# One-core hybrid decoder block: small weights side by side, score, split and evacuation steps reordered, and some of the last stage's stores and loads put on GpSimd's queue

## The chip, the cores and the metric

The kernel runs on one core of a Trainium2 chip. A core has TensorE (PE, matrix products; PEld is its weight load), VectorE (DVE), ScalarE (ACT), GpSimd (POOL) and SyncE (SP, which here only issues transfers). Each runs its own instructions in order and waits for the others by semaphores. Transfers issued from the queues of SP, ACT and POOL run on the same 16 DMA engines. The metric is the time of one execution in microseconds (us). Shapes below are partitions x elements.

## The reference

1040 tokens (16 meta tokens and 1024 of x) of width 1024 go through one layer, in float32:

```
h = h + mixer_block(rms_norm(h, norm_mix), ...)
h = h + conv_ffn(rms_norm(h, norm_ffn), w_up, conv_w, conv_b, w_down)
return rms_norm(h, norm_final)[16:]
```

mixer_block projects h with w_in into queries, keys and values of four GLA heads and four mLSTM heads, 24 small columns (g_lr, 16 wide, from which the GLA decay is made; m_i and m_f, 4 each), output gates and branch gates. A GLA head is gated linear attention, `scores[t,s] = sum_k q[t,k] k[s,k] exp(b[t,k] - b[s,k])` for s <= t, with b the running sum of the log decay, in chunks; an mLSTM head is a matrix memory with its own gates. The heads' outputs are normed, gated, multiplied with a branch weight each, merged and multiplied with w_out. conv_ffn is a gated MLP of width 2816 with a causal convolution of width 3 over tokens.

## The kernel before

Every float32 operand of a large product is split into a high part (a copy of ACT into float32r, H) and a low part (a subtraction of DVE or POOL, L); a product is three matmuls, HH, HL and LH, added up in PSUM. A scheduler places each engine's instructions by priorities (`hp`, and the order in which the code issues them); `tc.issue_after(x)` puts an instruction behind x.

**Projections and heads.** `key_query_proj(s)` and `value_proj(s)` give head s's matmuls (tiles pj and pv) in steps, and after each step `advance` lets the heads' own work (`gla`, `post`, ...) take a step. The 24 small columns come first: w_lr holds their weights, high and low apart, each padded to 128 columns; TensorE multiplies them in three thirds of the tokens by `proj_cm` (L160), three matmuls for each of 8 k, and ACT puts each third into raw_s with a bias. `pre` (L630) multiplies raw_s for the decay; DVE makes the running sums b (tile bc).

**Scores.** In `gla` the off-diagonal scores of a head are made in levels of block size b = 1, 2, ..., 64. `level(b)` builds a tile pk (differences on DVE, L742 and L743; Exp on ACT, L744; products on POOL and DVE, L746 and L747). `scores_small(pk, b)` multiplies it on TensorE (sc, L696), and DVE copies the result under a mask into A (L713). The list `made` keeps levels that were built and not yet multiplied: a level is multiplied when two newer ones are built. `diagonal` gives kq (L661), whose product with ones (L667) are the scores inside small blocks; sct (L686) turns A.

**Post.** `post(s, ...)` scales the head's output o, transposes it on TensorE (ot, L604), has ACT evacuate it to `of` (L606), and stores it. Head 0's post runs while head 1's levels are built.

**FFN up.** The up product goes over pairs q of 128 gate and 128 up columns and two pieces p of the tokens, in a Strassen-like scheme with 7 products on 2 x 2 blocks; `piece` (L1035 by way of `product`) adds them up in the banks V, X, Y and Z; u2raw (L1064) is the evacuation of X's sum on ACT. `prep_pair` splits the weights (A, L1451 and L1452, is one of its blocks). `combos(i)` builds the token blocks from hT: Br holds plain blocks, Bt the sums T; both are split (BH1r, BL1r, BH1t, BL1t: L1432 on ACT, L1433 on DVE; the 1 is the piece p = i // 2). `gate_pair(q)` convolves, gates and stores the result (rows adr, in sums for the down product), on SP's queue, for the last pair on ACT's.

**FFN down.** 44 steps i: round r (half of the tokens), phase ph (0: four products, 1: three), and row pair m. `fill(i)` loads a raw weight block (rd), its sums tdn, prepared earlier by POOL, and adr, and splits each into places do, dy, db, dw; `ahead` keeps four steps loaded ahead. All these loads go through `transfer`, which keeps them in order on SP's queue:

```
def transfer(dst, s):
    with tc.issue_after(queued[0].ins) if queued else nullcontext():
        queued[:] = [nc.sync.dma_start(dst, s)]
```

The four rows accs (4 x 128 x 1024) hold h (stored before as hsc) and take the sums from PSUM (DVE, L1780), half in `middle` behind phase 0, half in `finish` behind phase 1. `scaled` norms them: squares on ACT (sqj, L1796), the inverse root on POOL (fr, L1803), the product with gfin on DVE (L1808), the scaling on ACT (L1809), the store to out (L1811). Round 0's rows are scaled early in round 1 (`later`), before `load_acc(1)` loads the rows of round 1 into the same accs.

Of the kernel before, what the change touches and what calls it, by code (L numbers as in the profile page):

```python
# [45 lines left out]
def hybrid_kernel(ctx, tc, x, meta, norm_mix, w_in, b_in, gla_w_gate, gla_b_gate, gla_norm,  # L46
# [40 lines left out]

    rooted = []

# [24 lines left out]

    lr2 = hd.tile([P, 2, NK, P], F32R, name="w_lr", tag="v", bufs=2)
    nc.vector.memset(lr2.bitcast(F32), 0.0)
    lrHL = [lr2[:, i] for i in range(2)]
    SMALL = ((0, O_LR, 16), (32, O_MI, 4), (64, O_MF, 4))

    def prep_small():  # L120

        raw = wp.tile([P, T], F32, name="wr_lr", tag="gst", bufs=1)[:, :NK * 24].rearrange("p (k n) -> p k n", k=NK)
        wH, wL = lrHL
        at = 0
        for p0, off, n in SMALL:
            nc.sync.dma_start(raw[:, :, at:at + n], w_in[:, off:off + n].rearrange("(k p) n -> p k n", p=P))
            h = wH[:, :, p0:p0 + n]
            nc.scalar.activation(h, raw[:, :, at:at + n], AF.Copy)
            nc.vector.tensor_tensor(wL[:, :, p0:p0 + n], raw[:, :, at:at + n], h.bitcast(F32), OP.subtract)
            at += n  # L130
        return wH, wL

# [453 lines left out]
    def post(s, o, om, sc, ncols):  # L586
# [12 lines left out]
        for j in range(2):  # L599
            of = hd.tile([P, T], F32, name=f"of{s}_{j}", tag="r", bufs=2)  # L600
            for gi in range(2):
# [3 lines left out]
                a, b = 2 + 512 * gi, 2 + 512 * (gi + 1)  # L605
                nc.scalar.activation(of[:, a:b], tp.rearrange("p n w -> p (n w)"), AF.Copy, scale=ncols[j])  # L606
                if gi == 0:
# [35 lines left out]
    def gla(s):  # L643
# [74 lines left out]
        def level(b):  # L718
# [24 lines left out]
            nc.vector.tensor_tensor(pl, b4[:, :, 1, :], ref, OP.subtract)  # L743
            nc.scalar.activation(pk[:, :SEQ], pk[:, :SEQ], AF.Exp, scale=1.0 / 16)  # L744
            for eng, (e, k, _) in zip((nc.gpsimd, nc.vector), early):
# [670 lines left out]
    def combos(i):  # L1416

        p, c0 = i // 2, 128 * (i % 2) + (2 if i == 1 else 0)
        o, w = (0, 130) if i == 0 else (2, 128)
        A, B = hT[1 + i][:, :, o:130], hT[5 + i][:, :, o:130]  # L1420
        t12, t34 = (rb.tile([P, 8, 130], F32, name=f"T{g}_{i}", tag=f"T{g}")[:, :, :w] for g in (12, 34))
        nc.vector.tensor_tensor(t12[:, 0:4], B[:, 0:4], A[:, 0:4], OP.subtract)
        nc.vector.tensor_tensor(t12[:, 4:8], B[:, 4:8], t12[:, 0:4], OP.subtract)
        nc.vector.tensor_tensor(t34[:, 0:4], B[:, 4:8], B[:, 0:4], OP.subtract)
        nc.vector.tensor_tensor(t34[:, 4:8], A[:, 4:8], t12[:, 4:8], OP.subtract)
        jobs = ((Br, 0, 8, A), (Br, 8, 4, B[:, 4:8]), (Bt, 0, 8, t12), (Bt, 8, 8, t34))
        if i == 3:
            jobs = ((Br, 0, 8, A), (Bt, 0, 4, t12[:, 0:4]), (Bt, 8, 4, t34[:, 0:4]), (Bt, 4, 4, t12[:, 4:8]),
                    (Br, 8, 4, B[:, 4:8]), (Bt, 12, 4, t34[:, 4:8]))
        for dst, r0, n, src in jobs:  # L1430
            h = dst["H", p][:, r0:r0 + n, c0:c0 + w]
            nc.scalar.activation(h, src, AF.Copy)  # L1432
            x = nc.vector.tensor_tensor(dst["L", p][:, r0:r0 + n, c0:c0 + w], src, h.bitcast(F32), OP.subtract)  # L1433
            parts.append(x)

# [62 lines left out]
    def gate_pair(q):  # L1498
# [12 lines left out]
        m = q // 2  # L1511
        eng = nc.sync if q < NJ - 1 else nc.scalar

# [157 lines left out]

    def fill(i, pl, weights=True):

# [12 lines left out]
        jobs.append((pl.aH, pl.aL, pl.aL.bitcast(F32), (1024, 768)[ph], adr[ph][m][r].rearrange("p j c -> p (j c)")))  # L1686
        for h, l, raw, n, s in jobs:
            h, l, raw = h[:, :n], l[:, :n], raw[:, :n]
            if s is not None:
                transfer(raw, s)  # L1690
            nc.scalar.activation(h, raw, AF.Copy)
            nc.vector.tensor_tensor(l, raw, h.bitcast(F32), OP.subtract)
# [95 lines left out]
    def finish(r, j):  # L1788
# [17 lines left out]
        def scaled(i):  # L1806
# [3 lines left out]
            t = 4 * i + 2 * r + j  # L1810
            nc.sync.dma_start(out[P * t:P * (t + 1), :], acc[i])  # L1811

# [35 lines left out]

    AHEAD, PRI_F = 4, 100
    fetched = FIRST  # L1850
    kept = {}

    def ahead(i):
        nonlocal fetched
        while fetched < min(i + 1 + AHEAD, len(seq)):
            r, ph, m = seq[fetched]
            with hp(PRI_F):
                pl = ring[0](fetched)
                again = (r, ph) == (1, 0) and m in KEPT
                if again:  # L1860
                    pl.wH, pl.wL = kept[m]
                fill(fetched, pl, not again)
                used[fetched] = pl
# [12 lines left out]
    while i < len(seq):  # L1876
# [7 lines left out]
        if later and k == 2:  # L1884
# [51 lines left out]
```

## Time and profile before

| | |
|---|---|
| median of 3 runs | 1888.07 us (1885.97 to 1889.87) |
| profiled execution | 1888.81 us, its span 1887.1 us |
| busy | PE 1857.6 us, DVE 1217.3, ACT 869.0, POOL 403.5 |
| DMA | 270.02 MB in the span, mean 143 GB/s |

The profile's page has the busy time of each engine and its costliest groups; the list of waits says for which engine and line another one waited; windows give each engine's busy time, the granted clock of TensorE, the share of the DMA engines and GB/s in a stretch; timelines give start, duration, engine, line, operation, out<-in, and in brackets the idle time before and its releaser.

### The profile page before, as it was taken

To read this page: it belongs to the slowest core of one execution; us is meant where nothing else is said; L and a number is where in the kernel's file an instruction comes from. 1 tells how busy PE (TensorE), PEld (TensorE's weight loads), DVE (VectorE), ACT (ScalarE), POOL (GpSimd) and SP (SyncE) were. 2 spreads that over 40 slices of the span, in tenths; PEclk is the share of its full clock that TensorE was granted. 3 is DMA by queue.
4 is the path that set the end of the run, shared out by engine and by line. 5 is a ranking of instruction groups with operands and counts; after the bars stand their busy time and mean duration, and the time that the engine had idled before them with its cause. 6 is when DMAs were issued, how large, how long until landed. Compare 5 with 4: busy or idle time off the path is not lost.

```text
span 1887.1 us, 32610 instructions
## 1 busy us (share of the span) xinstructions
PE 1857.6 (98%) x13305; PEld 1775.2 (94%) x13305; DVE 1217.3 (65%) x1806; ACT 869.0 (46%) x1389; POOL 403.5 (21%) x447
## 2 busy tenths in 40 slices
PE   8999999999999999999999999999999999999998
PEld 8989999999999999999999999999999999987876
DVE  7666658454552465665442547688787887887767
ACT  5454555545553433432422335543443443455665
POOL 5401101205320001133281600012322222100100
PEclk9999999999999999999999999999999999999999
DMA  5211021143332856565983743324333334298794
GB/s 176 73 37 56 16 71 48 35 127 98 97 100 79 213 121 160 149 185 156 325 247 108 232 141 129 118 85 129 117 102 112 109 107 130 76 324 328 258 376 173
DMA packets 223361, 270.02 MB, mean 143 GB/s; under 512 B 13742, under 2 KB 179136, under 8 KB 223211
## 3 DMA queue, kind: packets, MB, share of 16 engines
q1 hardware_dynamic: 202907, 202.03, 34.8%
q0 software_dynamic: 16160, 55.65, 9.1%
q10 hardware_dynamic: 4144, 10.26, 1.6%
q8 instruction: 104, 1.70, 0.4%
q14 instruction: 46, 0.38, 0.1%
HBM read 198.33 MB, written 69.57 MB: 142 GB/s over the span
## 4 chain that ended last, share of the span: by engine, by line
PE 82%; DVE 7%; DMA 6%; ACT 2%; issue 2%; POOL 0%; SPq 0%; POOLq 0%; DVEq 0%; ACTq 0%
PE pj L163 11%; PE pv L206 7%; PE Xu L1035 6%; PE Yu L1035 6%; PE Zu L1035 6%; PE bg L1270 5%; PE bm L1270 5%; PE Xg L1035 4%; PE Yg L1035 4%; PE po L1557 4%; PE Zg L1035 4%; PE Vu L1035 3%; PE Vg L1035 2%; PE pdX L1712 1%; PE pdY L1712 1%
## 5 line engine op out<-in xcount | busy, mean ns | idle before, releaser
L513 POOL TENSOR_TENSOR ts<-ts 128x256 f32<-128x256 f32 x88 | 78.2, 894 | 49.4 <-DMA ts<-in_ffn_w_down_dram 47.0
L1470 POOL TENSOR_TENSOR SB<-SA,rg 128x512 f32<-128x512 f32 x20 | 31.8, 1588 | 238.0 <-issue 123.7
L206 PE MATMUL pv<-wH_mv,xH 128*128 128x256 f32 x256 | 74.8, 292 | 0.1
L206 PE MATMUL pv<-wH_gv,xH 128*128 128x256 f32 x256 | 74.4, 291 | 0.0
L746 POOL TENSOR_TENSOR pk<-pk,kT 128x256 f32<-128x256 f32 (+1 forms) x24 | 31.0, 1293 | 196.6 <-ACT pk L744 145.7
L1557 PE MATMUL po<-wH_wo,yH 128*128 128x256 f32 x256 | 72.7, 284 | 0.1
L206 PE MATMUL pv<-wL_gv,xH 128*128 128x256 f32 x256 | 72.1, 281 | 0.0
L206 PE MATMUL pv<-wL_mv,xH 128*128 128x256 f32 x256 | 72.0, 281 | 0.0
L206 PE MATMUL pv<-wH_mv,xL 128*128 128x256 f32 x256 | 72.0, 281 | 0.0
L1557 PE MATMUL po<-wL_wo,yH 128*128 128x256 f32 x256 | 71.7, 281 | 0.3 <-DVE wL_wo L112 0.3
L206 PE MATMUL pv<-wH_gv,xL 128*128 128x256 f32 x256 | 72.0, 281 | 0.0
L1557 PE MATMUL po<-wH_wo,yL 128*128 128x256 f32 x256 | 72.0, 282 | 0.0
L1505 DVE SCALAR_TENSOR_TENSOR cv<-u,fc,cv 128x1024 f32<-128x1024 f32 x44 | 65.2, 1485 | 0.4
L1452 POOL TENSOR_TENSOR A<-u2raw,A 128x512 fp32r<-128x512 f32 x20 | 43.8, 2192 | 90.4 <-ACT A L1451 90.4
L1270 PE MATMUL bg<-ogL,wH_bg 128*128 128x342 f32 x192 | 61.5, 320 | 0.0
L1270 PE MATMUL bm<-omH,wH_bm 128*128 128x342 f32 x192 | 61.4, 320 | 0.0
L1270 PE MATMUL bg<-ogH,wL_bg 128*128 128x342 f32 x192 | 61.4, 320 | 0.0
L1270 PE MATMUL bg<-ogH,wH_bg 128*128 128x342 f32 x192 | 61.4, 320 | 0.0
L1270 PE MATMUL bm<-omH,wL_bm 128*128 128x342 f32 x192 | 61.3, 319 | 0.0
L1270 PE MATMUL bm<-omL,wH_bm 128*128 128x342 f32 x192 | 61.2, 319 | 0.0
L1803 POOL TENSOR_TENSOR fr<-fv,mhalf 128x1 f32<-128x1 f32 x8 | 8.6, 1072 | 226.3 <-DVE fv L1800 137.4
L210 DVE TENSOR_TENSOR v<-pv,bB 128x256 f32<-128x256 f32 x64 | 26.7, 419 | 45.5 <-PE pv L206 45.1
(767 smaller groups left out, 7516.5 us busy)
## 6 DMA issues: line engine op xcount, KB each, us to landing
gw<-in_w_in_dram SPq DMA_DIRECT2D x26, 512.0 KB
ts<-in_ffn_w_down_dram POOLq DMA_DIRECT2D x44, 256.0 KB, 4.0
tdn<-ts POOLq DMA_DIRECT2D x44, 256.0 KB, 3.1
rg<-in_ffn_w_up_dram SPq DMA_DIRECT2D x22, 512.0 KB
ru<-in_ffn_w_up_dram SPq DMA_DIRECT2D x22, 512.0 KB
adr<-s SPq DMA_DIRECT2D x40, 256.0 KB
rd<-in_ffn_w_down_dram SPq DMA_DIRECT2D x20, 512.0 KB
do<-tdn SPq DMA_DIRECT2D x18, 512.0 KB
```

Of the source, the lines that this page charges most:

```text
L163: nc.tensor.matmul(pt[:, :n], a[:, k, :], b[:, k, base + t0:base + t0 + n], start=(i == 0), stop=(i == 3 * NK - 1))
L206: nc.tensor.matmul(pt[:, :DV], a[:, k, t0:t0 + P], b[:, k % 4, :], start=(i == 0), stop=(i == 3 * NK - 1))
L210: nc.vector.tensor_tensor(vt[:n, c, :DV], pt[:n, :DV], bB[:n, :], OP.add)
L513: nc.gpsimd.tensor_tensor(t[:, o], t[:, a], t[:, b], OP.subtract)
L746: eng.tensor_tensor(e, e, k, OP.mult)
L1035: nc.tensor.matmul(out[:, :n], x[:, k, :], y[:, k, :], start=start and k == 0 and j == 0, stop=stop and k == 3 and j == 2, skip_group_chec ...
L1270: nc.tensor.matmul(pt[:, i, :n], a[:, k, :], b[k][:, base + t0:base + t0 + n], start=(k == 0 and j == 0), stop=(k == NK - 1 and j == 2))
L1452: eng.tensor_tensor(l, src, h.bitcast(F32), OP.subtract)
L1470: late.tensor_tensor(sb[:, 0:4], sa[:, 0:4], rg[:, 0:4], OP.subtract)
L1505: nc.vector.scalar_tensor_tensor(y, u[:, j:SEQ + j], fc[:, j, jj:jj + 1], y, OP.mult, OP.add)
L1557: nc.tensor.matmul(pt[:, :DV], a, b[:, k % 4, :], start=(k == 0 and i == 0), stop=(k == NK - 1 and i == len(terms) - 1))
L1712: nc.tensor.matmul(banks[r, j, b], p, q, start=first and k == 0, stop=last and k == 2, skip_group_check=True)
```

## The change

- **Small weights**: w_lr is one tile with the high parts in columns 0 to 63 and the low parts in 64 to 127 (`small_proj`). For each k one matmul of all 128 columns with xH gives both products, one of the first 64 with xL the third. ACT copies the lower half of PSUM to raw_s, DVE adds the upper half and the bias. m_f's four rows move from 64 to 36, and a transfer on POOL's queue copies them to 64.
- **Scores**: for s = 0 a level is multiplied when three newer ones are built.
- **Exponentials**: for head 1 the Exp of the levels stands behind head 0's evacuation `of`.
- **Combos**: for piece 1 the plain block A is split before the sums T are built.
- **Queues**: the last pair's stores go to POOL's queue instead of ACT's; gfin is loaded after the second kept step of round 1 instead of in round 0; in round 0 accs is loaded one row per fill (steps 7 to 10); in round 1 accs is loaded on POOL's queue, and round 0's rows are stored to out there.

```
-    lr2 = hd.tile([P, 2, NK, P], F32R, name="w_lr", tag="v", bufs=2)
+    lr2 = hd.tile([P, NK, P], F32R, name="w_lr", tag="v", bufs=2)
...
-    SMALL = ((0, O_LR, 16), (32, O_MI, 4), (64, O_MF, 4))
+    SMALL = ((0, O_LR, 16), (32, O_MI, 4), (36, O_MF, 4))
...
+    def small_proj():
+
+        U.get(uk["lr"])
+        for t0, n in TH_ALL:
+            pt = ps.tile([P, 512], F32, name=f"plr{t0}", tag="pj", bufs=3)
+            for k in range(NK):
+                first, both = (xL, 64), (xH, P)
+                for j, (x, m) in enumerate((both, first) if k < NK - 1 else (first, both)):
+                    nc.tensor.matmul(pt[:m, :n], lr2[:, k, :m], x[:, k, t0:t0 + n],
+                                     start=(k == 0 and j == 0), stop=(k == NK - 1 and j == 1), skip_group_check=True)
+            with hp(PRI_E):
+                r = raw_s[0:64, t0:t0 + n]
+                nc.scalar.activation(r, pt[64:128, :n], AF.Copy)
+                nc.vector.scalar_tensor_tensor(r, pt[0:64, :n], bsm[0:64], r, OP.add, OP.add)
+            yield
+        nc.gpsimd.dma_start(raw_s[64:68, :], raw_s[36:40, :])
...
-                yield from proj_cm(uk["lr"], TH_ALL, 0, lambda p, t0, n: nc.scalar.activation(
-                    raw_s[0:96, t0:t0 + n], p[0:96, :], AF.Identity, bias=bsm[0:96]))
+                yield from small_proj()
...
-                nc.scalar.activation(of[:, a:b], tp.rearrange("p n w -> p (n w)"), AF.Copy, scale=ncols[j])
+                flipped[s] = nc.scalar.activation(of[:, a:b], tp.rearrange("p n w -> p (n w)"), AF.Copy,
+                                                  scale=ncols[j]).ins
...
-            nc.scalar.activation(pk[:, :SEQ], pk[:, :SEQ], AF.Exp, scale=1.0 / 16)
+            with tc.issue_after(flipped[0]) if s == 1 and 0 in flipped else nullcontext():
+                nc.scalar.activation(pk[:, :SEQ], pk[:, :SEQ], AF.Exp, scale=1.0 / 16)
...
-            if len(made) > 2:
+            if len(made) > (3 if s == 0 else 2):
                 c, pk = made.pop(0)
                 scores_small(pk, c)
             yield
+        if len(made) > 2:
+            c, pk = made.pop(0)
+            scores_small(pk, c)
...
+        def block(dst, r0, n, src):
+            h = dst["H", p][:, r0:r0 + n, c0:c0 + w]
+            nc.scalar.activation(h, src, AF.Copy)
+            x = nc.vector.tensor_tensor(dst["L", p][:, r0:r0 + n, c0:c0 + w], src, h.bitcast(F32), OP.subtract)
+            parts.append(x)
+
+        if p:
+            block(Br, 0, 8, A)
...
+        if i == 2:
+            jobs = jobs[1:]
         if i == 3:
-            jobs = ((Br, 0, 8, A), (Bt, 0, 4, t12[:, 0:4]), (Bt, 8, 4, t34[:, 0:4]), (Bt, 4, 4, t12[:, 4:8]),
+            jobs = ((Bt, 0, 4, t12[:, 0:4]), (Bt, 8, 4, t34[:, 0:4]), (Bt, 4, 4, t12[:, 4:8]),
                     (Br, 8, 4, B[:, 4:8]), (Bt, 12, 4, t34[:, 4:8]))
...
-        eng = nc.sync if q < NJ - 1 else nc.scalar
+        eng = nc.sync if q < NJ - 1 else nc.gpsimd
...
-        for h, l, raw, n, s in jobs:
+        for at, (h, l, raw, n, s) in enumerate(jobs):
+            if amid and at == len(jobs) - 1:
+                amid()
...
-    def load_acc(r):
-        for j in range(2):
-            for i, t in enumerate((2 * r + j, 4 + 2 * r + j)):
-                transfer(acc_of(r, j)[i], hsc[t])
+    def load_acc(r, load, n):
+        j, i = divmod(n, 2)
+        return lambda: load(acc_of(r, j)[i], hsc[4 * i + 2 * r + j])
...
-            nc.sync.dma_start(out[P * t:P * (t + 1), :], acc[i])
+            (nc.sync if r else nc.gpsimd).dma_start(out[P * t:P * (t + 1), :], acc[i])
...
-                fill(fetched, pl, not again)
+                fill(fetched, pl, not again, load_acc(0, transfer, fetched - ACC_AT) if 0 <= fetched - ACC_AT < 4 else None)
+                if again and m == KEPT[-1]:
+                    transfer(gfin, rowb(norm_final, 0, D))
...
-        if i == FIRST:
-            with hp(PRI_D):
-                nc.sync.dma_start(gfin, rowb(norm_final, 0, D))
-        if ph == 0 and k == 5:
+        if (r, ph, k) == (1, 0, 5):
             with hp(PRI_F):
-                load_acc(r)
+                for n4 in range(4):
+                    load_acc(r, nc.gpsimd.dma_start, n4)()
```

How the instructions move, at three places. ACT at the start of the up stage, before; Xu_0 is the bank that the next products wait for, A_0 a weight block whose load comes late:

```order
L1432 ACTIVATE BH1r<-hT_12540 128x8x128
L1432 ACTIVATE BH1t<-T_2_12459 128x8x128
L1451 ACTIVATE A_0_12505<-u2raw 128x512
L1064 ACTIVATE u2raw<-Xu_0_12511 128x258
L1414 ACTIVATE hT_12592<-htp_0_12593 128x4x128
```

The same place after:

```order
L1442 ACTIVATE BH1r<-hT_12520 128x8x128
L1442 ACTIVATE BH1t<-T_2_12438 128x8x128
L1442 ACTIVATE BH1t<-T_2_12439 128x8x128
L1082 ACTIVATE u2raw<-Xu_0_12491 128x258
L1476 ACTIVATE A_0_12485<-u2raw 128x512
L1432 ACTIVATE hT_12572<-htp_0_12573 128x4x128
```

The evacuation of Xu_0 now stands ahead of A_0. DVE a little later, before; hT_12540 is the plain block that the first products of piece 1 (Vu_1) read, the T are its sums:

```order
L1452 TENSOR_TENSOR A_0_12505<-u2raw,A_0_12505 128x512
L1071 TENSOR_TENSOR ug_12508<-Yu_0_12512,u2raw 128x256
L1422 TENSOR_TENSOR T_3_12605<-hT_12592,hT_12540 128x4x128
L1424 TENSOR_TENSOR T_3_12606<-hT_12592 128x4x128
L1072 TENSOR_TENSOR uu_12509<-Zu_0_12513,u2raw 128x258
L1423 TENSOR_TENSOR T_3_12605<-hT_12592,T_3_12605 128x4x128
L1433 TENSOR_TENSOR BL1r<-hT_12540,BH1r 128x8x128
```

and after:

```order
L1477 TENSOR_TENSOR A_0_12485<-u2raw,A_0_12485 128x512
L1089 TENSOR_TENSOR ug_12488<-Yu_0_12492,u2raw 128x256
L1443 TENSOR_TENSOR BL1r<-hT_12520,BH1r 128x8x128
L1090 TENSOR_TENSOR uu_12489<-Zu_0_12493,u2raw 128x258
L1448 TENSOR_TENSOR T_3_12585<-hT_12572,hT_12520 128x4x128
L1450 TENSOR_TENSOR T_3_12586<-hT_12572 128x4x128
```

The split of the plain block moved ahead of four instructions. SP's queue in round 1 before, where rd, db and dy are loads of the coming steps:

```order
L1670 DMA dy_31_18730<-adr_11186 128x1024
L1670 DMA accs<-hsc 128x1024 x2
L1811 DMA out_dram<-accs 128x1024 x2
L1670 DMA accs<-hsc 128x1024 x2
L1670 DMA rd_18770<-in_ffn_w_down_dram 128x2x512
L1670 DMA db_18769<-tdn_425 128x1024
```

and POOL's queue after, from the last pair's stores on:

```order
L1540 DMA adr_11166<-s_17643 128x2x256 x2
L1540 DMA adr_11167<-s_17644 128x2x256 x2
L1829 TENSOR_TENSOR fr_18581<-fv_18578,mhalf 128x1
L1837 DMA out_dram<-accs 128x1024
L1829 TENSOR_TENSOR fr_18589<-fv_18586,mhalf 128x1
L1837 DMA out_dram<-accs 128x1024
L1803 DMA accs<-hsc 128x1024
L1829 TENSOR_TENSOR fr_18597<-fv_18594,mhalf 128x1
L1829 TENSOR_TENSOR fr_18605<-fv_18602,mhalf 128x1
L1803 DMA accs<-hsc 128x1024
L1837 DMA out_dram<-accs 128x1024 x2
L1803 DMA accs<-hsc 128x1024 x2
```

The loads of accs and the stores to out have left SP's queue for POOL's, where the roots fr of the third and fourth row stand behind the first load.

More of the change, by code (lines that the diff above doesn't have):

```diff
@@ L86, in hybrid_kernel @@
     nc.scalar.activation(warm, one1, AF.Exp)
-    rooted = []
+    rooted, flipped = [], {}
     def rstd_of(ss, n, w, pool, name):
@@ L113, in prep @@
         return wH, wL
-    lr2 = hd.tile([P, 2, NK, P], F32R, name="w_lr", tag="v", bufs=2)
+    lr2 = hd.tile([P, NK, P], F32R, name="w_lr", tag="v", bufs=2)
     nc.vector.memset(lr2.bitcast(F32), 0.0)
-    lrHL = [lr2[:, i] for i in range(2)]
-    SMALL = ((0, O_LR, 16), (32, O_MI, 4), (64, O_MF, 4))
+    SMALL = ((0, O_LR, 16), (32, O_MI, 4), (36, O_MF, 4))
     def prep_small():
         raw = wp.tile([P, T], F32, name="wr_lr", tag="gst", bufs=1)[:, :NK * 24].rearrange("p (k n) -> p k n", k=NK)
-        wH, wL = lrHL
         at = 0
@@ L126, in prep_small @@
             nc.sync.dma_start(raw[:, :, at:at + n], w_in[:, off:off + n].rearrange("(k p) n -> p k n", p=P))
-            h = wH[:, :, p0:p0 + n]
+            h = lr2[:, :, p0:p0 + n]
             nc.scalar.activation(h, raw[:, :, at:at + n], AF.Copy)
-            nc.vector.tensor_tensor(wL[:, :, p0:p0 + n], raw[:, :, at:at + n], h.bitcast(F32), OP.subtract)
+            nc.vector.tensor_tensor(lr2[:, :, 64 + p0:64 + p0 + n], raw[:, :, at:at + n], h.bitcast(F32), OP.subtract)
             at += n
-        return wH, wL
+    def small_proj():
[13 more added lines that the diff above has]
+        nc.gpsimd.dma_start(raw_s[64:68, :], raw_s[36:40, :])
     def wsrc(w, k0, nk, n0, n):
@@ L1426, in combos @@
         jobs = ((Br, 0, 8, A), (Br, 8, 4, B[:, 4:8]), (Bt, 0, 8, t12), (Bt, 8, 8, t34))
+        if i == 2:
+            jobs = jobs[1:]
         if i == 3:
-            jobs = ((Br, 0, 8, A), (Bt, 0, 4, t12[:, 0:4]), (Bt, 8, 4, t34[:, 0:4]), (Bt, 4, 4, t12[:, 4:8]),
+            jobs = ((Bt, 0, 4, t12[:, 0:4]), (Bt, 8, 4, t34[:, 0:4]), (Bt, 4, 4, t12[:, 4:8]),
                     (Br, 8, 4, B[:, 4:8]), (Bt, 12, 4, t34[:, 4:8]))
[L1430 to L1434, printed above, removed]
+        for job in jobs:
+            block(*job)
     nth = 0
@@ L1670, in transfer, with fill @@
             queued[:] = [nc.sync.dma_start(dst, s)]
-    def fill(i, pl, weights=True):
+    def fill(i, pl, weights=True, amid=None):
         r, ph, m = seq[i]
@@ L1847, in finish @@
         nc.sync.dma_start(out[P * t:P * (t + 1), hi], fo[:, hi])
-    AHEAD, PRI_F = 4, 100
+    AHEAD, PRI_F, ACC_AT = 4, 100, 7
     fetched = FIRST
```

## The prediction

> **What bounds it now.** I read the page's first part, the waits of TensorE, and then windows and timelines at each place where it waits. The page:
>
> ```profile
> PE 1857.6 (98%) x13305; PEld 1775.2 (94%) x13305; DVE 1217.3 (65%) x1806; ACT 869.0 (46%) x1389; POOL 403.5 (21%) x447
> ```
>
> TensorE is the bound; of the span of 1887.1 us it is idle for 29.5. So the change can win in two ways: fewer matmuls, or waits of TensorE that go without another one coming in their place. TensorE's waits that the change touches (total us, times, longest):
>
> ```profile
> PE pdV L1712 <- ACT db L1691: 1.9, 1, 1.9
> PE ot L604 <- ACT of L606: 1.6, 1, 1.6
> PE Xu L1035 <- ACT u2raw L1064: 1.5, 1, 1.5
> PE sc L696 <- DVE A L713: 1.5, 1, 1.5
> PE Vu L1035 <- DVE BL1r L1433: 1.1, 1, 1.1
> PE sc L696 <- DVE pk L747: 1.0, 1, 1.0
> ```
>
> They add up to 8.6 us, at four places; two shorter ones follow in part 5. The sum below is against the profiled run's own 1888.8 us; the median of the runs shown, 1888.07, is 0.7 lower. A measurement of this kernel can tell about 0.2%, 3.8 us, from no change.
>
> **1. Small weights side by side.** The tile w_lr before:
>
> ```profile
> L163 PE MATMUL pj<-xH,w_lr x48: 314/322/327, 42.2 to 53.5; 128*128 128x346 f32 x32, 128*128 128x348 f32 x16
> L163 PE MATMUL pj<-xL,w_lr x24: 316/322/327, 42.3 to 53.3; 128*128 128x346 f32 x16, 128*128 128x348 f32 x8
> ```
>
> 72 matmuls start from 42.2 to 53.5, so one every 11.3/71 = 0.159 us. 48 remain: 24 x 0.159 = **-3.8**. Of these 48, 24 now have weights of 64 columns and alternate with weights of 128. No row shows that alternation; the nearest is one that goes from 128 columns to 16, to 2 and back:
>
> ```profile
> 393.82 0.32 PE L163 MATMUL pj<-xH,wH_mq 128*128 128x348 f32 x1
> 393.98 0.27 PE L579 MATMUL rtp<-ident,srst 128*16 128x128 f32 x1
> 394.09 0.27 PE L580 MATMUL rtp<-ident,srst 128*2 128x128 f32 x1
> 394.12 0.41 PE L163 MATMUL pj<-xL,wH_mq 128*128 128x348 f32 x1
> 394.36 0.32 PE L163 MATMUL pj<-xH,wL_mq 128*128 128x348 f32 x1
> ```
>
> From 393.98 to 394.36 are 0.38 us for two narrow matmuls and a wide one; the wide one alone takes 0.16 and a transpose of full width 0.11 ((0.60 - 0.27)/3 in the row of 165.08 below), together 0.38 for one and two. So narrowing costs nothing there. The row that speaks against it changes the rows used, from 128 to 2:
>
> ```profile
> 165.08 0.60 PE L604 MATMUL ot<-ident,or 128*128 128x128 f32 x4
> 165.61 0.22 PE L616 MATMUL otm<-ident,om 2*128 2x2 f32 x1
> ```
>
> The fourth ot starts at 165.08 + 3 x 0.11 = 165.41 and otm 0.20 later: 0.09 lost. With some 46 changes of width that would be 46 x 0.09 = 4.1 us, and the term +0.3. I take -3.8, by the row that also keeps 128 rows; bounds -3.8 and +0.3. The Trainium skill (TensorEngine Tiling (Array Packing), Key Properties) says that a change of the tiling mode drains TensorE; if 64 columns count as a mode of their own, the second price holds. The trace shows such a drain at otm and none at rtp.
>
> The new ACT copy and DVE add per third lie where ACT and DVE stand nearly idle (the columns after the width are PE, PEld, DVE, ACT and POOL busy, then clock, DMA share and GB/s):
>
> ```profile
> 42.00:54.00 12.00, 12.00 (x79) 12.00 (x78) 0.00 (x0) 1.72 (x4) 10.60 (x9) 1.00 0.26 88
> ```
>
> Between the last third and the matmul that reads it stand 24 other matmuls, about 3 us; without that cover they would cost about 1. The DVE chain of the first head starts after this window, so it moves forward with the matmuls. The copy of four rows that is added to GpSimd's queue stands behind its token sums and is read only three heads later; clearing w_lr is half as long, at the very start: both 0.
>
> **2. First head's scores a step later.** The two waits on A and pk (2.5 us) go, but DVE is full there, and what the diagonal scores wait for stands at the end of its work:
>
> ```profile
> 80.00:100.00 20.00, 17.83 (x137) 16.27 (x136) 19.34 (x34) 6.65 (x8) 7.44 (x4) 1.00 0.02 7
> ```
> ```profile
> 97.62 0.68 DVE L661 TENSOR_TENSOR kq<-An,kq 128x512 fp32r<-128x512 f32 x1
> ```
>
> DVE is busy 19.34 of 20 us. The end of kq at 98.30 isn't moved by the order of matmuls: TensorE arrives earlier and waits there instead. **0**; bounds -0.7 (the 0.66 us in which DVE is idle) and +1.0 (the scores for 32 now stand just behind an ACT evacuation).
>
> **3. Exponentials of head 1 behind head 0's evacuation.** Head 0's evacuation stood behind this exp, before which ACT was idle for 2.81 us, waiting for its input:
>
> ```profile
> 159.16 1.06 ACT L744 ACTIVATE pk<-pk 128x1024 f32<-128x1024 f32 x1 [2.81 <-DVE pk L743]
> ```
>
> Put ahead, the evacuation runs in that idle time and the exp is not later for it. The ot wait goes: **-1.6**; bounds -1.6 and 0 (if DVE's next step of head 1 then ends last).
>
> **4. Blocks without sums first.** TensorE at the start of the FFN's up stage and what it waited for:
>
> ```profile
> 1220.00:1224.00 4.00, 2.71 (x18) 2.34 (x19) 3.23 (x7) 2.51 (x5) 0.00 (x0) 1.00 0.00 0
> 1224.00:1228.00 4.00, 2.51 (x16) 1.91 (x16) 3.97 (x8) 1.86 (x3) 0.00 (x0) 1.00 0.23 66
> 1228.00:1232.00 4.00, 4.00 (x23) 4.00 (x22) 2.70 (x6) 1.02 (x2) 0.00 (x0) 0.58 0.00 0
> 1232.00:1236.00 4.00, 4.00 (x36) 4.00 (x35) 3.97 (x7) 0.83 (x1) 0.00 (x0) 1.00 0.01 2
> ```
> ```profile
> 1220.25 0.63 ACT L1451 ACTIVATE A<-u2raw 128x512 fp32r<-128x512 f32 x1 [1.61 <-DMA u2raw<-in_ffn_w_up_dram]
> 1220.78 0.37 ACT L1064 ACTIVATE u2raw<-Xu 128x258 f32<-128x258 f32 x1
> ```
> ```profile
> 1226.18 1.22 DVE L1433 TENSOR_TENSOR BL1r<-hT,BH1r 128x1024 fp32r<-128x1024 f32 x1
> ```
>
> ACT stood 1.61 us before A for a load, with the evacuation of Xu behind it; the order now has the evacuation first. And BL1r, which ended at 1227.4, comes four DVE instructions earlier, and those ahead of it lose their wait for Xu's evacuation; I estimate 3 us, which is when TensorE arrives. So 1.5 + 1.1 = 2.6 us of waits go, less 0.5 that I take to come back: Zu needs A's lower part from DVE, whose start still follows the load. Then the clock: 0.58 in the third row, where 23 matmuls start against 36 in the next, (36 - 23) x 4/36 = 1.4 us. I take it that it doesn't fall when the waits are gone: -2.1 - 1.4 = **-3.5**; bounds -4.0 and -0.9 (the chain through A keeps TensorE waiting and the clock falls anyway). The Trainium skill (TensorE: Matmul & The Clock Gate, What's actually happening) lets the clock halve only after an idle window of about 3.4 us. No wait here is longer than 1.5, so the trace doesn't bear that out as stated; by it the fall would have another cause and the 1.4 would stay, and the sum be 1.4 less.
>
> **5. Down stage, round 0.** What TensorE waited for, SyncE's wait for a store that ACT issued, and four loads in a row:
>
> ```profile
> PE pdV L1712 <- ACT dy L1691: 0.6, 1, 0.6
> ```
> ```profile
> PE pdV L1712 <- DVE db L1692: 0.5, 1, 0.5
> ```
> ```profile
> SPq L1670 <- DMA adr<-s: 6.6, 1, 6.6
> ```
> ```profile
> 1696.48 5.25 SPq L1670 DMA_DIRECT2D accs<-hsc  x4
> ```
>
> The last pair's stores no longer stand among ACT's splits; SyncE doesn't wait 6.6 us for one (on GpSimd only the root calculations of round 1 stand behind them, 90 us later); gfin goes to a later stretch, and accs go one per fill. The waits pdV on dy and db, 0.6 + 0.5, go: **-1.1**; bounds -1.1 and 0 (the DMA engines are simply full).
>
> **6. Down stage, round 1.** SyncE waited up to 21.7 us to store a row and 8.1 for a store to land, and the loads behind came late:
>
> ```profile
> SPq L1811 <- ACT accs L1809: 30.7, 4, 21.7
> ```
> ```profile
> SPq L1670 <- DMA out_dram<-accs: 8.9, 2, 8.1
> ```
> ```profile
> 1803.78 10.57 DMA out_dram<-accs
> ```
> ```profile
> 1812.00:1816.00 4.00, 4.00 (x19) 3.27 (x18) 0.00 (x0) 0.00 (x0) 0.00 (x0) 1.00 0.65 219
> 1816.00:1820.00 4.00, 4.00 (x19) 3.29 (x18) 0.00 (x0) 0.00 (x0) 0.00 (x0) 1.00 0.83 270
> ```
>
> ACT and DVE have nothing to split there, and TensorE then waits 1.9. The DMA engines leave 0.35 x 4 + 0.17 x 4 = 2.1 us free, enough: **-1.9**; bounds -1.9 and the rival below.
>
> **7. Tail.** The last squares now stand behind a scaling of ACT, up to 1.15 us:
>
> ```profile
> 1877.35 1.15 ACT L1809 ACTIVATE accs<-accs,fr 128x1024 f32<-128x1024 f32 x1 [0.30 <-POOL fr L1803]
> ```
>
> **+0.5**; bounds 0 and 1.2.
>
> **Sum.** -3.8 + 0 - 1.6 - 3.5 - 1.1 - 1.9 + 0.5 = -11.4: profiled 1877.4, median 1876.7.
>
> **Rivals.**
> - *Changes of width drain TensorE* (term 1): +4.1, so 1880.8. For it otm, against it rtp.
> - *DVE paces both early places.* If the first head's chain doesn't start earlier, term 1 is eaten by the wait for kq, and with A's lower part holding Zu term 4 is -0.9: 1876.7 + 3.8 + 2.6 = 1883.1; with term 5 at 0, 1884.2. For it: DVE's 19.34 of 20. Against: it was idle from 42 to 54.
> - *GpSimd's queue holds ACT* (slower). In round 1 the load of accs waits on GpSimd until the first store of out has landed, and the next two root calculations (fr) stand behind it; ACT stands before its scaling, and the splits of the next weights stand behind ACT.
>
> ```profile
> 1785.80 2.33 SPq L1811 DMA_DIRECT2D out_dram<-accs  x2
> ```
> ```profile
> 1802.14 0.85 PE L1712 MATMUL pdV<-db 128*128 128x512 f32 x3
> ```
>
> From the landing I estimate 9 us to the last split: two fr, two scalings, three splits on ACT and one on DVE, each at the 1.15 of the scaling above. TensorE needs it at 1802.1, and the store was issued at 1785.8: a landing of up to 1802.1 - 9 - 1785.8 = 7.3 us is free, 10.57 as above costs 3.3 (1880.0). It ends slower than before from a landing of 7.3 + 11.4 = 18.7 us; at 21.7, as long as SyncE's longest wait, it costs 14.4 and gives 1891.1. Against it: loads and stores of this size that GpSimd issued landed sooner:
>
> ```profile
> h<-in_x_dram POOLq DMA_DIRECT2D x2, 512.0 KB, 3.8
> ```
>
> **How the numbers follow.** My forecast, with the bounds of its terms 1872 to 1880, 0.55; drain 0.17; DVE-paced 0.18, about half of it within 0.2%; GpSimd's queue 0.10, counted as slower with all else that goes wrong. Faster: 0.55 + 0.17 + 0.08 = 0.80; same 0.10; slower 0.10. The range reaches from 1871 over the drain and DVE-paced cases to 1886, and leaves out the last rival.
>
> **What would show it.** Right: w_lr at 48 matmuls 0.159 apart; no wait of Xu, Vu and ot; clock 1.00 through the start of the up stage; SyncE without waits on accs or out. Wrong: starts of w_lr over 0.2 apart; a longer wait of sct or sc at 93 to 97; ACT waiting several us for fr near 1775; pdV or db waits in the down stage of the old size.

## The result, and the profile after

The changed kernel took 1879.3 us (median of 6 runs, 1877.62 to 1883.32); the kernel before, run beside it, 1888.32 (6 runs, 1885.97 to 1890.68). The ratio is 0.9955, 95% interval 0.9941 to 0.9969: 9 us faster. The profiled run took 1879.94 with a span of 1878.2, against 1888.81 and 1887.1.

The first part of the page, to be laid beside that of before:

```profile
PE 1852.3 (99%) x13281; PEld 1769.6 (94%) x13281; DVE 1223.1 (65%) x1809; ACT 867.7 (46%) x1389; POOL 413.8 (22%) x462
```

24 matmuls are gone, and TensorE's busy time is down by 5.3 us; its idle time went from 29.5 to 25.9. The waits of TensorE after (total us, times, longest):

```profile
PE sct L700 <- DVE A L727: 4.7, 2, 4.3
PE pdV L1739 <- DVE db L1719: 0.7, 1, 0.7
PE pdZ L1739 <- DVE accs L1806: 0.7, 2, 0.4
PE sc L710 <- POOL pk L761: 0.7, 1, 0.7
PE pdY L1739 <- DVE accs L1806: 0.6, 1, 0.6
PE pdV L1739 <- DVE dy L1719: 0.5, 1, 0.5
PE Xu L1053 <- ACT u2raw L1082: 0.4, 1, 0.4
```

The waits on `of` (1.6) and on BL1r (1.1) are gone, that on u2raw is 0.4 in place of 1.5, and for db 0.7 and 0.2 are left of the 1.9. New at the top is a single wait of 4.3 us in the first head.

**Where the time went, by stage.** The start of one and the same matmul is compared in two traces. An example is the first of the ot group, 165.08 before and

```profile
161.82 0.60 PE L617 MATMUL ot<-ident,or 128*128 128x128 f32 x4
```

after: 3.26 us earlier. Such differences at the ends of the stages, less those at their starts, give the table (us against the profiled run of before, minus is a gain). The columns are: the start up to 21 us; small projections and first head, to 120; the ot wait, to 161; the up stage's start, 1215 to 1400; round 0 of the down stage, 1703 to 1720; round 1, 1720 to 1856. The kernels are described below; the first two have the code of before in the last four columns.

| kernel | start | first head | ot | up | round 0 | round 1 |
|---|---|---|---|---|---|---|
| scores only | +0.28 | +2.35 | 0.00 | -1.57 | -0.19 | +0.77 |
| weights only | +0.29 | -2.74 | 0.00 | -2.39 | +3.01 | -2.36 |
| **changed** | -0.44 | -0.97 | -1.85 | -3.83 | -1.77 | -0.51 |
| changed, again | +0.37 | -0.44 | -1.85 | -3.64 | -1.77 | -2.48 |
| scores back | -0.29 | -2.58 | -1.85 | -3.82 | -1.77 | -0.75 |
| scores back, again | +0.28 | -2.63 | -1.86 | -3.70 | -1.78 | -0.37 |
| SyncE in round 1 | -0.72 | -1.07 | -1.86 | -2.73 | -1.77 | -0.55 |
| no order for the exp | -0.48 | +0.22 | 0.00 | -3.63 | -1.77 | -2.23 |
| block of 3 late | -0.75 | -0.93 | -1.86 | -0.87 | -1.77 | -1.91 |
| loads last | +0.41 | -0.58 | -1.85 | -3.72 | -1.77 | -1.58 |
| both | +0.62 | -2.69 | -1.86 | -3.62 | -1.77 | -1.58 |
| both, again | -0.07 | -2.69 | -1.85 | -3.53 | -1.78 | -1.77 |

The row of the changed kernel sums to -9.37; between the stages 0.5 is lost again (+0.28 from 161 to 1215 and +0.22 from 1400 to 1703), and behind 1856 nothing changes: -8.9, the difference of the spans. Where several traces of one code stand in a column, they show how far one trace can be trusted: to 0.1 us at ot and in round 0 of the changed code, and only to some 2 us in round 1. The reference is one trace, too: the code of before differs among its three traces by 2.4 us at the up stage and by some 3 in each round.

**The first head.** TensorE and DVE after:

```profile
93.25 0.70 DVE L727 COPY_PREDICATED A<-mu,sc 128x512 f32<-128x512 uint8 x1
94.98 0.68 DVE L675 TENSOR_TENSOR kq<-An,kq 128x512 fp32r<-128x512 f32 x1
94.01 1.69 PE L700 MATMUL sct<-A,flip 128*128 128x512 f32 x2 [4.28 <-DVE A L727]
```
```profile
92.00:96.00 4.00, 1.99 (x4) 1.05 (x5) 4.00 (x8) 0.77 (x2) 0.00 (x0) 0.80 0.00 0
96.00:100.00 4.00, 3.92 (x24) 3.25 (x23) 3.12 (x5) 3.49 (x7) 0.00 (x0) 0.77 0.00 0
```

The end of kq came forward from 98.30 to 95.66, by 2.6 us where the projections came forward by 4.3 (the run with the weights alone shows where the rest went). But the scores that used to stand in this stretch come a step later, and TensorE has nothing to run until DVE has done the mask copy at 93.25. The granted clock then falls to half for 3.4 us (0.80 and 0.77 in the two rows), and 24 matmuls start in four microseconds instead of 36.

**The start of the up stage** after, the same four stretches as before:

```profile
1220.00:1224.00 4.00, 4.00 (x32) 3.80 (x33) 3.90 (x7) 1.56 (x4) 0.00 (x0) 1.00 0.26 70
1224.00:1228.00 4.00, 4.00 (x35) 3.95 (x34) 4.00 (x8) 1.02 (x2) 0.00 (x0) 1.00 0.01 2
1228.00:1232.00 4.00, 4.00 (x32) 3.63 (x31) 3.63 (x8) 1.72 (x3) 0.00 (x0) 1.00 0.09 26
1232.00:1236.00 4.00, 4.00 (x36) 4.00 (x35) 2.87 (x4) 2.01 (x2) 0.00 (x0) 1.00 0.60 175
```

TensorE is filled, with 32 to 36 matmuls in each, where the first three had 16 to 23, and the clock stays at 1.00.

**Round 1 of the down stage** after, on GpSimd, ACT and TensorE:

```profile
1777.89 0.59 POOL L1837 DMA_DIRECT2D out_dram<-accs  x1 [1.48 <-ACT accs L1835]
1787.80 0.54 POOL L1803 DMA_DIRECT2D accs<-hsc  x1 [6.40 <-issue]
1788.36 1.08 POOL L1829 TENSOR_TENSOR fr<-fv,mhalf 128x1 f32<-128x1 f32 x2
1788.96 1.15 ACT L1835 ACTIVATE accs<-accs,fr 128x1024 f32<-128x1024 f32 x1 [6.54 <-POOL fr L1829]
1794.05 0.73 PE L1739 MATMUL pdV<-db 128*128 128x512 f32 x2 [0.17 <-ACT db L1718]
1795.50 0.50 PE L1739 MATMUL pdV<-db 128*128 128x512 f32 x1 [0.71 <-DVE db L1719]
```

The load into accs can go out only when the store of the same buffer has landed. That store was issued at 1777.89 and took 9.4 us to land; the load went out 0.5 us later. The roots (fr) stand behind it on GpSimd, ACT's scaling behind them, and ACT's and DVE's splits of db behind that; TensorE waits 0.17 + 0.71 for those. This is the chain of the rival "GpSimd's queue holds ACT", at a small price.

### The profile page after: what moved, and what is told of

The parts are those of the page before. It is cut to its first block, busy times and chain, and to the rows that moved or that the text cites. A ratio compares the mean times of both kernels' runs of the same rounds, so it can differ in the third digit from the quotient of the medians.

```text
span 1878.2 us, 32585 instructions
## 1 busy us (share of the span) xinstructions
PE 1852.3 (99%) x13281; PEld 1769.6 (94%) x13281; DVE 1223.1 (65%) x1809; ACT 867.7 (46%) x1389; POOL 413.8 (22%) x462
## 3 DMA queue, kind: packets, MB, share of 16 engines
q0 software_dynamic: 17824, 61.44, 10.1%
## 4 chain that ended last, share of the span: by engine, by line
PE 88%; DVE 5%; DMA 3%; ACT 2%; issue 1%; POOL 0%; SPq 0%; POOLq 0%; ACTq 0%; DVEq 0%
PE pj L177 11%; PE pv L220 8%; PE Yu L1053 6%; PE Xu L1053 6%; PE Zu L1053 6%; PE bg L1288 5%; PE bm L1288 5%; PE Zg L1053 4%; PE Yg L1053 4%; PE Xg L1053 4%; PE po L1582 4%; PE Vu L1053 3%; PE pdZ L1739 3%; PE pdX L1739 2%; PE pdY L1739 2%; PE Vg L1053 2%
## 5 line engine op out<-in xcount | busy, mean ns | idle before, releaser
L1476 ACT ACTIVATE HA<-rg 128x1024 fp32r<-128x1024 f32 x16 | 17.0, 1061 | 72.7 <-PE Yu L1053 72.3
```

## The experiments

**Scores back at their old step** (the changed kernel otherwise):

```
-            if len(made) > (3 if s == 0 else 2):
+            if len(made) > 2:
...
-        if len(made) > 2:
-            c, pk = made.pop(0)
-            scores_small(pk, c)
         yield
         kq = [diagonal(g) for g in range(2)]
```

> The changed kernel with the first head's scores at their old step. Theory A (the deferral turned several short waits into one of 4.28 us, by making the diagonal scores wait for a mask copy that DVE does late, and the clock then halved for 3.4 us): the first head's end stands 3.1 us ahead of before, as DVE's chain does, against 1.4 now; total -1.7 against the changed kernel, 1877.6; waits of sc of 0.5 to 1.5 us as before, clock 1.00. Rival (the small weights' gain is eaten by DVE in any order): the first head's end stays 1.4 ahead, total 1879.3.

1877.97 us (4 runs, 1877.18 to 1879.35), 0.9946 (0.9929 to 0.9962) of the kernel before. Its waits in the first head are the old ones:

```profile
PE sc L710 <- DVE A L727: 1.5, 1, 1.5
PE sc L710 <- DVE pk L762: 1.1, 1, 1.1
PE sc L681 <- DVE kq L675: 0.5, 1, 0.5
```
```profile
89.11 0.73 DVE L727 COPY_PREDICATED A<-mu,sc 128x512 f32<-128x512 uint8 x1
```

The second fence is the mask copy that sct needs, on DVE: it ends at 89.84, where in the changed kernel it ended at 93.95 and TensorE waited for it. The clock stays at 1.00 there, and the first head gains 2.58 us in place of 0.97. **The scores a step later alone**, on the kernel before (the same edit the other way round):

> The kernel before with only the deferral of the first head's scores. Theory A: slower than before by 1 to 2 us; one wait of sct of 3 to 4 us in the place of four waits of 3.1 us together; if it is longer than about 3.4 us, TensorE's clock is near 0.5 for 3.4 us behind it, else it costs under 1 us and the clock stays at 1.00. Rival (deferral is neutral alone, the loss comes with the narrower small weights): head's end within 0.3 us of before.

1890.35 us (one run), 2.35 us lost in the first head; the sct wait and the stretches around it:

```profile
PE sct L686 <- DVE A L713: 4.1, 2, 3.7
```
```profile
96.00:100.00 4.00, 2.69 (x4) 1.50 (x5) 3.38 (x7) 1.47 (x2) 0.00 (x0) 0.50 0.00 0
100.00:104.00 4.00, 4.00 (x23) 3.69 (x22) 3.59 (x4) 2.80 (x7) 0.00 (x0) 0.67 0.00 0
```

So this part of the change, added to either kernel, loses about 2 us there: one long wait takes the place of several short ones, and the clock halves behind it, here for 6.8 us.

**Loads last.** In round 1 the summed rows are loaded behind the first pair's roots on GpSimd:

```
-            nc.gpsimd.tensor_tensor(rs, v, mhalf, OP.pow)
+            rooted[:] = [nc.gpsimd.tensor_tensor(rs, v, mhalf, OP.pow)]
...
-            with hp(PRI_F):
+            with hp(PRI_F), tc.issue_after(rooted[0].ins):
                 for n4 in range(4):
```

> The changed kernel with round 1's loads of accs put behind the last root calculation on GpSimd's queue. Theory A (GpSimd waits 6.4 us for a store to land with two roots behind it, so ACT, DVE and then TensorE wait): ACT's wait of 6.5 us for fr goes, TensorE's waits of 0.2 and 0.7 for db go, 0.9 us faster than the changed kernel: 1878.4. Rival (the DMA engines, at a share of 1.03 there, bring the weights late in any order): the waits stay, or move to loads (rd, db), total within 0.3 of 1879.3. Against both: accs arrive later and the sums behind phase 0 wait for them: slower.

1880.96 us (4 runs, 1878.4 to 1881.36), 0.9958 (0.9941 to 0.9974). The pdV waits of round 1 are gone and the stage gains 1.58, but the total is no better than the changed kernel's. In this trace the first head gains 0.58 only, the clock being at half for 6.8 us, and a wait of 1.1 us at 1012 stands in no other.

**Both** (scores back, loads last):

> Both of the edits above in the changed kernel: scores at their old step and loads of accs behind the last root. If both theories hold, -1.7 - 0.9: 1876.7; by the rivals 1879.3.

1876.92 us (6 runs, 1875.82 to 1878.17), 0.9939 (0.9925 to 0.9953).

**SyncE in round 1**: the summed rows and round 0's stores of out on SyncE's queue again.

```
-            (nc.sync if r else nc.gpsimd).dma_start(out[P * t:P * (t + 1), :], acc[i])
+            nc.sync.dma_start(out[P * t:P * (t + 1), :], acc[i])
...
-                    load_acc(r, nc.gpsimd.dma_start, n4)()
+                    load_acc(r, transfer, n4)()
```

> The changed kernel with the second round's summed rows and the first round's last pair of stores of out back on SyncE's queue. Theory (SyncE's wait for a row to be scaled held the weights' loads; the move took that away, but GpSimd's queue then held the root behind a landing of some 9.5 us, so that 0.45 us were left of the 1.9 forecast): SyncE again waits some 20 us for accs in the second round, TensorE waits 1.9 to 2.7 us in sum for pdV and pdY there, and the stage from 1720 to 1856 us is 0.5 to 1.5 us longer than with the change as it is, the span 1878.7 to 1879.7. Rival (the move between queues was worth nothing; the DMA engines are simply full there): the same waits as with the change, 0.88 us for pdV and 0.58 for pdY, and the stage within 0.2 us of it.

1880.02 us (one run). SyncE's waits are the old ones, and pdV waits once:

```profile
SPq L1837 <- ACT accs L1835: 31.3, 4, 22.1
SPq L1695 <- DMA out_dram<-accs: 9.3, 2, 8.5
```
```profile
PE pdV L1739 <- ACT db L1718: 1.0, 1, 1.0
```

Round 1 gains 0.55, as in the changed kernel's first trace. The theory's loss of 0.5 to 1.5 isn't seen against that trace; against the mean of the six traces with the changed code in round 1 (-1.38, from -0.37 to -2.48) it would be 0.8. One trace can't settle it.

**No order for head 1's exponentials**:

```
-            with tc.issue_after(flipped[0]) if s == 1 and 0 in flipped else nullcontext():
+            with nullcontext():
```

> The changed kernel without the exponentials of head 1 put behind head 0's evacuation. Theory (ACT's order alone held of): the wait of ot is back at about 1.6 us, and the gain of 1.86 us between the first head's end and 161 us is gone; everything later shifts by 1.6 to 1.9 us, the span 1879.8 to 1880.1. Rival (in the new order of the first head the wait had gone anyway, because the first head ends 2.9 us later against TensorE's other work): no wait of ot over 0.5 us, span within 0.5 us of 1878.2.

1881.02 us (one run), span 1879.3. The wait is back, and the column ot reads 0.00 in place of -1.85:

```profile
160.59 0.66 PE L617 MATMUL ot<-ident,or 128*128 128x128 f32 x4 [1.64 <-ACT of L619]
```

The theory holds. The span is 0.5 to 0.8 under what it gave: against the changed kernel's first trace the first head gained 1.2 less, and round 1 1.7 more.

**Block of combination 3 late**: only combination 2 splits its block without sums first.

```
-        if p:
+        if i == 2:
             block(Br, 0, 8, A)
...
-            jobs = ((Bt, 0, 4, t12[:, 0:4]), (Bt, 8, 4, t34[:, 0:4]), (Bt, 4, 4, t12[:, 4:8]),
+            jobs = ((Br, 0, 8, A), (Bt, 0, 4, t12[:, 0:4]), (Bt, 8, 4, t34[:, 0:4]), (Bt, 4, 4, t12[:, 4:8]),
```

> The changed kernel with the block without sums first only in combination 2, combination 3 in the old order. Theory (each of the two waits was ended by its own reordering): Vu waits again, 1.1 us for BL1r or for the block of combination 3, Xu at most 0.4, and the gain of 3.8 us at the up stage's start falls by 1.1 where the clock stays at 1.00, by 2.5 where it halves for 3.4 us: after the start of the up stage the lead over the kernel before is 5.7 or 4.3 us in place of 6.8. Rival (combination 2's block alone frees DVE and ACT for combination 3, too): Vu waits under 0.3 us and the lead stays at 6.5 to 6.8.

1880.63 us (one run). Vu waits again, and the clock falls again:

```profile
PE Vu L1053 <- DVE BL1r L1443: 1.2, 1, 1.2
```
```profile
1220.00:1224.00 4.00, 2.52 (x14) 1.91 (x13) 3.96 (x7) 2.41 (x4) 0.00 (x0) 0.90 0.23 66
1224.00:1228.00 4.00, 4.00 (x26) 4.00 (x25) 2.11 (x5) 0.39 (x1) 0.00 (x0) 0.67 0.00 0
```

The up stage gains 0.87 in place of 3.83: 3.0 us hang on combination 3's order, 1.2 of them the wait, and the rest is the clock's: 0.10 x 4 + 0.33 x 4 = 1.7 in the two rows.

**Weights only**: the kernel before with the small weights side by side.

```
-                yield from proj_cm(uk["lr"], TH_ALL, 0, lambda p, t0, n: nc.scalar.activation(
-                    raw_s[0:96, t0:t0 + n], p[0:96, :], AF.Identity, bias=bsm[0:96]))
+                yield from small_proj()
```

> The kernel before with the small weights side by side and nothing else of the change. Theory (24 matmuls go and the narrow ones cost no more; DVE's work of the first head starts earlier by as much): 48 matmuls of w_lr 0.160 us apart, a lead of 3.8 to 4.2 us behind the projections, 2.6 to 3.1 of it left behind the first head's scores, where waits of 0.5 to 1.2 us on A, pk and kq remain; the rest of the kernel as before, with its waits of 1.6 for ot, 1.5 and 1.1 at the up stage's start; span 1883.8 to 1885.0, 1.4 less or more by whether the clock halves there. Rival (DVE paces the first head and its chain does not start earlier): the lead falls to under 0.5 us by the end of the first head's scores, span 1886.6 to 1887.1.

1884.61 us (one run), span 1882.9: 3.9 us ahead behind the projections (3.61 against the kernel before, and 0.29 of start), of which 2.74 are left behind the first head. The theory's numbers hold there. Where the other 1.2 go can be seen on DVE and GpSimd. The kernel before, its last token sum on GpSimd and the running sum b on DVE:

```profile
59.23 1.30 POOL L482 TENSOR_TENSOR xa<-xa,xb 128x514 f32<-128x514 f32 x1
63.97 2.32 DVE L640 TENSOR_TENSOR_SCAN bc<-rmask,la 128x1040 f32<-128x1040 f32 x1
```

and this run:

```profile
59.53 2.18 POOL L495 TENSOR_TENSOR xa<-xa,xb 128x514 f32<-128x514 f32 x1
60.58 3.31 DVE L653 TENSOR_TENSOR_SCAN bc<-rmask,la 128x1040 f32<-128x1040 f32 x1
```

DVE's running sum and the step ahead of it (1.46 us in place of 1.24) now run beside GpSimd's token sum, which had been done 2.2 us before them, and all three take longer: on DVE 1.2 us together. It is so in all eleven traces with the small weights and in neither of the two without. The token sum ends 1.2 us after the step ahead of the running sum, at 61.71, and the running sum 2.2 after that, at 63.89: about as long as each takes alone, as if each had waited for the one before to end. That is read from these rows; no run keeps the two engines apart.

The rest of this trace shows what the kernel before's code can do by itself:

```profile
1224.00:1228.00 4.00, 4.00 (x36) 4.00 (x35) 3.97 (x8) 1.02 (x2) 0.00 (x0) 1.00 0.01 2
```
```profile
PE pdV L1725 <- ACT dy L1704: 2.1, 1, 2.1
PE Vu L1048 <- DVE BL1r L1446: 1.1, 1, 1.1
PE Xu L1048 <- ACT u2raw L1077: 0.5, 1, 0.5
```

At the up stage the wait for u2raw is 0.5 in place of 1.5, without any edit there, and the clock stays at 1.00 behind the same wait of 1.1 for Vu, while in round 0 the wait on dy is 2.1 in place of 0.6, and the clock halves there.

**Three kernels on one chip**, 5 runs each: the changed kernel, the one with the scores back, and both edits.

> The changed kernel once more, beside the next two on one chip. Traces of the same code in the second round so far differ by up to 1.7 us there, and the first head's end by up to 1.3 us with the place of the 3.413-us windows in which the clock is set; so 1878 to 1881 us.

> The changed kernel with the first head's scores at their old step, beside the changed kernel on the same chip. Theory (the later step adds one wait of 3.2 to 4.3 us for sct in place of 1.2 to 2 us of shorter ones, and the clock halves behind it for 3.4 or 6.8 us): 1.4 to 2.9 us under the changed kernel, median 1876.5 to 1878.5. Rival (the traces happened to fall so): within 0.7 us of it.

> The same with the second round's summed rows loaded behind the first pair's roots on GpSimd. Theory (GpSimd's queue holds the roots in the changed kernel): another 0.8 to 1.2 us under the kernel with the scores at their old step. Rival (the stage differs as much from run to run, and the place of the loads is worth nothing): within 0.7 us of it, either way.

Changed: 1878.88 (1878.27 to 1881.07), 0.9950 (0.9936 to 0.9963). Scores back: 1879.09 (1876.42 to 1880.12), 0.9944 (0.9932 to 0.9957). Both: 1876.90 (1876.73 to 1878.89), 0.9940 (0.9927 to 0.9952). With all runs of each code, on different chips, the means are 1879.5 (11 runs), 1878.2 (9) and 1877.2 (11). The changed kernel's second trace has the clock at half for 6.8 us:

```profile
92.00:96.00 4.00, 1.12 (x3) 0.61 (x3) 4.00 (x6) 0.63 (x1) 0.72 (x1) 0.61 0.00 0
96.00:100.00 4.00, 4.00 (x16) 3.01 (x14) 3.12 (x6) 2.61 (x3) 0.00 (x0) 0.54 0.00 0
```

The scores at their old step are worth 1.6 to 2.2 us in the first head, in every pair of traces; in the totals 1.3 by the means of all runs, and on this chip 0.9 by the means and nothing by the medians.

Part of it is lost again in round 1. Of the six traces with the changed code there, the three with the smaller lead over the kernel before at 1720 (5.6 to 7.5 us) gained 1.9 to 2.5 in that stage, the three with the larger (8.4 to 10.0) 0.4 to 0.75; in the two traces of this chip 2.2 more in the first head stand against 2.1 less in round 1. With the loads last the stage gave 1.6 to 1.8 at leads of 6.4, 9.2 and 10.1.

That the loads behind the roots are worth another microsecond isn't shown by the totals: with the scores back the means differ by 1.0 for it, without by 0.9 against it (1880.4, 4 runs, to 1879.5). That fits the leads: the loads' place would pay where TensorE comes early. But the traces are few, and why the lead matters isn't shown.

What the loads' place does is seen in the traces. With both edits, GpSimd's roots no longer wait for a landing:

```profile
1782.31 0.57 POOL L1834 DMA_DIRECT2D out_dram<-accs  x1 [1.48 <-ACT accs L1832]
1782.91 0.57 POOL L1826 TENSOR_TENSOR fr<-fv,mhalf 128x1 f32<-128x1 f32 x1
1784.95 0.58 POOL L1800 DMA_DIRECT2D accs<-hsc  x1 [1.48 <-issue]
```
```profile
PE pdY L1736 <- DVE accs L1803: 0.8, 1, 0.8
```

pdV then doesn't wait, and pdY waits 0.8 for the rows that come later. Both edits together are the best version found: 11.0 and 12.1 us under the medians of the kernel before on the two chips, and 2.0 under the changed kernel's on the one they shared, though its interval against the kernel before overlaps the changed kernel's.

## Why the prediction came out as it did

1876.7 was forecast and 1879.3 measured, inside the range of 1871 to 1886, and faster as the forecast was. Against the sum of -11.4 the profiled run shows -8.9. The small difference is in part luck: the first head fell 2.8 short of the forecast and round 1 1.4, while terms 3, 4, 5 and 7 gave 1.75 more than forecast and the start another 0.44, for which no term stood. The low end of the range doesn't come from the terms: their best bounds add up to -13.1, a median of 1875.0.

- **Term 1, -3.8: right for the matmuls.** These are the small projections after (calls, ns least, median and most, first and last start):

```profile
L138 PE MATMUL plr<-xH,w_lr x24: 314/320/327, 41.7 to 49.2; 128*128 128x346 f32 x16, 128*128 128x348 f32 x8
L138 PE MATMUL plr<-xL,w_lr x24: 314/321/327, 41.9 to 49.0; 128*64 128x346 f32 x16, 128*64 128x348 f32 x8
```

  48 matmuls from 41.7 to 49.2 are 7.5/47 = 0.160 us apart, against 0.159 before; 3.89 us are gained behind them. What didn't hold is that DVE's chain "moves forward with the matmuls": it lost 1.2 us of that beside GpSimd's token sum (weights only, above). The rival of the drain is out. The Trainium skill (TensorEngine Tiling (Array Packing), Key Properties) would have a change of mode drain TensorE; alternating between 64 and 128 columns on all 128 rows shows no drain.
- **Term 2, 0 with +1.0 as its worst: the step that failed.** It held that the end of kq "isn't moved by the order of matmuls: TensorE arrives earlier and waits there instead". The first half was near: less each trace's start, kq ends 0.35 to 0.5 us later with the scores a step later than with them at their old step. The second half was wrong. TensorE waits at sct, 4.28 us, for a mask copy that the later step puts some 4 us later on DVE, and has nothing else to run meanwhile; behind it the clock halves. That costs 1.6 to 2.2 (2.35 on the kernel before); it isn't the wait for the scores for 32 that the bound had. With the scores at their old step 2.6 to 2.7 of the 3.9 us survive. The clock was priced at the up stage and forgotten here, though the prediction named "a longer wait of sct or sc at 93 to 97" as the sign of being wrong.
- **Term 3, -1.6: right**, 1.85 in every trace with the order, none without it.
- **Term 4, -3.5: right in size against the trace of before** (-3.83). But the clock's fall, 1.4 of it, was a matter of that one trace: the same code gave 1.57 and 2.39 us back in two others without any edit there, with the clock at 1.00, and in the second of them Xu waited 1.0 less. And in the trace of the late block the clock fell behind a wait of 1.2. The late block shows what combination 3's order is worth; no run takes combination 2's order back.
- **Term 5, -1.1: right against the trace of before, a little low**: 1.77 or 1.78 in every trace with the change. The code of before lost another 3.0 there in the weights-only trace, and no run takes the three edits to the queues apart.
- **Term 6, -1.9: not shown.** The changed code gave 0.37 to 2.48, mean 1.38; the code of before -2.36 to +0.77 against its own first trace, mean -0.53, so the move is worth some 0.8 by the means, less than the spread. Nor do SyncE's waits by themselves make TensorE wait. The weights-only trace has them, with the code of before,

```profile
SPq L1824 <- ACT accs L1822: 29.9, 4, 21.8
SPq L1683 <- DMA out_dram<-accs: 8.3, 2, 7.5
```

  and pdV doesn't wait there in round 1, to which TensorE came with 3.0 us lost just ahead, in round 0. The rival's chain on GpSimd is real, and so was its sign, ACT waiting 6.5 us for fr. Where the first store landed 9.4 us after its issue (above), pdV waited 0.9, and 0.7 where it took 9.0; where it took 6.7 to 7.3, nothing (though in one of these four traces pdY waited 1.6), as here in the changed kernel's second trace, where it took 6.9:

```profile
1776.51 0.59 POOL L1837 DMA_DIRECT2D out_dram<-accs  x1 [1.48 <-ACT accs L1835]
1783.97 0.54 POOL L1803 DMA_DIRECT2D accs<-hsc  x1 [2.76 <-PE pdZ L1739]
```

  So its free landing was about right (forecast 7.3), but 9.4 cost 0.9, not the 2.1 that its formula gives, and 18.7 was never near. The 3.8 us held against it were those of a load at the kernel's start, and no store here landed as soon.
- **Term 7, +0.5: nothing** was lost behind 1856.
- **The rival of DVE's pace**, 1883 to 1884, is out as it was put, since the weights alone keep 2.74 of their lead; but 1.2 of 3.9 did go on DVE.

What stays open: whether the move from SyncE to GpSimd in round 1 is worth anything (0.8 by one trace against the mean of six, and by the means above), and why the start differs by up to 1.4 us between traces (column 1).

## What to carry to other kernels

Work taken out of a stretch in which TensorE waits anyway isn't free when it is put behind that stretch: it was what split one long wait into short ones. Price a wait of TensorE with the clock behind it, and take that price from several traces of the kernel before, since one trace has it or hasn't. When work moves forward in time, look at what it now runs beside: 1.2 of 3.9 us went where DVE came to run beside GpSimd. In these traces a load issued on GpSimd's queue held what GpSimd computes behind it until the buffer's store had landed, 6.7 to 9.4 us, so put it behind the small steps on which others wait.

## What the runs showed of the clock

The falls of the granted clock lie on a fixed grid: in the changed kernel's trace they begin at 9.10 and 94.44 us, 25 x 3.413 apart, in that of the late block at 93.40 and 1223.21, 331 x 3.413 apart, and each lasts one window of 3.413 us or two (three at the very start; that at the very end is cut by the end of the trace). The Trainium skill (TensorE: Matmul & The Clock Gate, What's actually happening) has a free-running window of 3413 ns, and the traces agree. The prediction read that as one unbroken wait of 3.4 us and found none; it is the window that counts, not the wait. Adding up TensorE's idle time in each window of that grid, over the ten traces that show it: after each of the seven windows at full clock in the first head with 2.2 to 3.4 us idle, in one wait or several, the next was at half, as it was after 2.05 us in round 0 of the weights-only trace. After 1.4 to 1.7 us it was so in two (1.49 in the trace of before at 1225, 1.48 in that of the late block at 1220) and not in six. Less than that never did it at full clock. So idle time alone doesn't decide between 1.4 and 1.7 us, and the same waits can halve the clock or not. In the trace of before the wait of 1.5 for Xu lay in one window and nothing followed, while the 0.2 and 1.1 for Zu and Vu shared another with 0.1 more, and the clock halved behind it. In the trace of the scores alone the grid cuts between those waits, so that the most idle of these windows had 1.2 us, and the clock stayed. Where the grid falls is luck of each run, worth about 1.4 us here.
